# Four token tiles turned by block transposes and a trip through DRAM instead of by TensorE, in a decoder layer on one core

## The chip, the core and the metric

The kernel runs on one core of a Trainium2 chip. The metric is the time of one execution on the device in microseconds (us); it is the median of several runs, all on the same chip. The profile is of one further execution of the same program, taken by the hardware profiler. Engines are named as in the profile: PE is TensorE's matmul, PEld its loading of weights, DVE is VectorE, ACT is ScalarE, POOL is GpSimd and SP is SyncE, which in this kernel issues most transfers.

## The reference

One layer over 1040 tokens (16 meta tokens and 1024 others) of width 1024, all in float32. The part around the change is the end of the token mixing and the start of the FFN:

```python
mixed = jax.nn.sigmoid(g_attn) * y_attn + jax.nn.sigmoid(g_conv) * y_conv
h = layer_norm(DEEPNORM_ALPHA * h + mixed @ w_out, ln1_g, ln1_b)
up = causal_dwconv(h @ ffn_w_up, ffn_dw, ffn_dw_b)
u, g = jnp.split(up, 2, axis=-1)
f = (jax.nn.gelu(g, approximate=False) * u) @ ffn_w_down
return layer_norm(DEEPNORM_ALPHA * h + f, ln2_g, ln2_b)
```

`mixed @ w_out` and the layer norm give rows of tokens; `h @ ffn_w_up` needs the same h with the 1024 features on partitions. So every 128 x 1024 tile of tokens has to be turned between the two.

## The kernel before, in words

**Products.** Every float32 matmul is made of three matmuls of a high and a low part (`product`, lines 325, 329 and 330). The FFN's two large products are formed by a scheme of seven products over 2 x 2 blocks, so the inputs of `h @ ffn_w_up` are sums and differences of four quadrants of h: DVE forms them (line 1285), ACT casts the high part of each (line 1276), and DVE subtracts to get the low part (line 1281).

**The w_out stage** is a loop over eight token tiles in the order 3, 7, 2, (-1), 6, 0, 4, 1, 5, where -1 is a pair of tokens at the edge. `out_rows(i)` makes the two halves of 512 columns of tile i: 24 matmuls into a PSUM bank `ps_w`, then on DVE the residual is added (line 1339) and half of the layer norm's statistics is taken (line 1340). After the second half come the statistics (lines 261, 268 on ACT, 276 to 278) and the normalising (line 1361). The rows are stored to `h1d`, since the last layer norm needs them; they live in two buffers of `RT` (the first half of `OB`), and the rows of h for the next tile (`h0d`) are loaded into the buffer that has come free.

**The turn.** `turn(i)` is called while a later tile is in its matmuls: eight PE transposes of 128 x 128 (line 1375) go into two PSUM banks behind the last matmul of a given half (`behind=[last]` fixes that place on PE), and eight ACT instructions (line 1385) take each 128 x 128 block out of PSUM, scale and shift it by the layer norm's gain and bias, and put it into its place of `FA`. Tile 3 is turned after the second half of tile 7, and each other tile after the first half of the tile behind it: tile 7 in tile 2, tile 2 in tile 6, tile 6 in tile 0, tile 0 in tile 4, tile 4 in tile 1, tile 1 in tile 5, and tile 5 after the stage. Below, "turn 4" is the turning of tile 4, and so on.

**Interleaved work.** The first weights of the FFN are split in the same stretch (ACT line 1405, DVE line 1406, sums on DVE line 1423), and the quadrants of the second half of the tokens (tiles 2, 3, 6, 7) are summed from tile 0 on. Every engine takes its instructions strictly in the order in which they stand in its program. That order is written: `line` chains DVE's work from tile 0 on, `rank` gives priorities, `after` pins single instructions.

**SP's queue** holds, in this stretch, a load of `h0d` and a store of `h1d` for each tile, two loads of four-byte pieces for the edge, and the weights. SP waits in its queue for what a transfer needs, and whatever is behind waits too.

Of the kernel before, what the change touches and what calls it, by code (L numbers as in the profile page):

```python
# [23 lines left out]
F = mybir.dt.float32  # L24
R = mybir.dt.float32r
AF = mybir.ActivationFunctionType
# [3 lines left out]
P = 128  # L30
D = 1024
KC = D // P
# [92 lines left out]
def tile_hybrid_layer(  # L125
# [3 lines left out]
    nc = tc.nc  # L129
    PSUM = bass.MemoryType.PSUM  # L130

    def dram(ap, offset, dims):
        return bass.AP(tensor=ap.tensor, offset=ap.offset + offset, ap=[list(d) for d in dims])

    def load(o, i):
        return nc.sync.dma_start(out=o, in_=i)
# [5 lines left out]
    def f32(ap):  # L142
        return ap.bitcast(F)

    def after(ins, first):

        tc.add_manual_dep(ins.ins, first.ins.name, mybir.DependencyInfo(
            mybir.DependencyClass.NoSync, mybir.DependencyReason.SCHED_ONLY), reason="order of work")

    @contextmanager  # L150
    def rank(p):

        saved = tc.cur_priority
        tc.cur_priority = p
        yield
        tc.cur_priority = saved
# [19 lines left out]
    h0d = dpool.tile([U, D], F, name="h0d")  # L176
# [1046 lines left out]
    def h1F(sub, h, k):  # L1223
        o = h1_at(sub, h * KC + k)
        return FA[:, o:h1_at(sub, h * KC + k + 1)]
# [85 lines left out]

    WO_ORDER = (4, 5, 0, 1, 2, 3, 6, 7)
    edge = const.tile([P, KC, 2], F, name="edge")
    r_next = [1]

    def out_rows(i, between=(), work=()):


        n, u = (P, 2 + i * P) if i >= 0 else (2, 0)
        if n == P:  # L1320
            o = r_next[0] % 2 * 1024
            r_next[0] += 1
            whole = RT[:, o:o + 1024]
            load(whole, h0d[u:u + n, :])
        else:
            whole = OB[:, 3072:4096]
        r = whole[:n]
        order = WO_ORDER if i != 5 else (0, 1, 2, 3, 6, 7, 4, 5)
        turned = None
        st = small.tile([P, 2, 6], F, name="st")  # L1330
        pin = line if i in (0, 4, 1, 5) else lambda ins: ins
        for half in range(2):
            hs = slice(half * 512, half * 512 + 512)
            ps = pat.tile([P, 512], F, name="ps_w", tag="mm", bufs=3)
            if n == P:
                last = product(ps, [(mixed(i, k, 0), mixed(i, k, 1), wo[k][0][:, hs], wo[k][1][:, hs])
                                    for k in order], turned)
                with rank(RK_TURN):
                    pin(nc.vector.tensor_tensor(r[:, hs], ps, r[:, hs], OP.add))
                    pin(nc.vector.bn_stats(st[:, half], r[:, hs]))  # L1340
                turned = None
                if between[half:] and between[half]:
                    turned = turn(*between[half], behind=[last])
                if half == 0:
                    for f, *x in work:
                        f(*x)
                continue

            for j in range(4):
                nc.tensor.matmul(ps[:2], sel[:, j // 2 * 2:j // 2 * 2 + 2], two_parts[j // 2][j % 2][:, hs],  # L1350
                                 start=j == 0, stop=j == 3)
            nc.scalar.copy(r[:, hs], ps[:2])
        if n < P:
            q = FA[:2, 0:1024]
            load(q, h0d[0:2, :])
            nc.vector.tensor_tensor(r, r, q, OP.add)
        with rank(RK_TURN):
            (mu, rs), = ln_stats([(r, n)], half_stats=st if n == P else None)
            for a in (512, 0) if i == 5 else (None,):
                x = r if a is None else r[:, a:a + 512]  # L1360
                ins = pin(nc.vector.tensor_scalar(x, x, mu, rs, OP.subtract, OP.mult))
        if n == P:
            load(h1d[u - 2:u - 2 + P, :], r)
        else:
            load(ed, r)
            for t in range(2):
                load(edge[:, :, t], dram(ed, t * D, [[1, P], [P, KC]]))
        return whole, n, ins

    def turn(i, r, n, ins, banks=None, behind=None, upper=False):  # L1370
        with rank(RK_TURN):
            for j, k0 in enumerate((4, 0) if upper else (0, 4)):
                ps = banks[j] if banks else pat.tile([P, 512], F, name="ps_h", tag="s", bufs=2)
                for k in range(4):
                    ins = nc.tensor.transpose(ps[:, k * P:(k + 1) * P], r[:, (k0 + k) * P:(k0 + k + 1) * P], ident)
                    if behind:
                        after(ins, behind[-1])
                        behind.append(ins)
                for k in range(k0, k0 + 4):
                    src = ps[:, (k - k0) * P:(k - k0 + 1) * P]  # L1380
                    h, jj = divmod(i, 4)
                    sub = 0 if jj < 2 else 1
                    a = 2 + jj * P - SUB[sub][0]
                    dst = h1F(sub, h, k)[:, a:a + P]
                    nc.scalar.activation(dst, src, AF.Identity, bias=b1col(k), scale=g1col(k))
        return behind[-1] if behind else None


    RING = [RHO[:, i * 1024:(i + 1) * 1024] for i in range(4)]
    RING += [None] * 4  # L1390
# [85 lines left out]
            5: [(w_first, 6)]}  # L1476
    for i in (3, 7, 2, -1, 6, 0, 4, 1, 5):
        if i == -1:
            out_rows(i)
            continue  # L1480
        rows = out_rows(i, ahead, work.get(i, ()))
        ahead = [None, (i, *rows)] if i == 3 else [(i, *rows)]
        if i == 3:
            two_rows(7, rows[2])
        if i == 7:
            for a, (hi, lo) in zip(two_sum, two_parts):
                after(split(a, hi, lo, True), rows[2])
            two_stack.close()
            W2.append(wo_stack.enter_context(tc.tile_pool(name="w2", bufs=1, side="right", reuse_waits="tile")).tile(
                [P, 2048], R, name="W2"))  # L1490
        if i == 0:
            form_t2(1)
        if i == 4:
            split_of(1, BT4)
            split_of(1, BT1)
            edges()
        if i == 1:
            split_of(1, BT3)
            split_of(0, B21, EARLY)
            form_t3(0, EARLY)  # L1500
            form_t4(0, EARLY)
# [427 lines left out]
```

## Time and profile before

| | |
|---|---|
| median of 3 runs | 1234.82 us (1234.75 to 1234.85) |
| the profiled execution's own time | 1234.65 us |
| its span, first to last instruction | 1232.9 us |
| PE busy, share of the span | 1223.6 us, 99% |
| DVE busy | 1084.5 us, 88% |
| ACT busy | 584.4 us, 47% |
| the w_out stage in the trace | about 500 to 588 us |
| granted TensorE clock, mean | 0.998 |

The profiled execution's time is 1.75 us longer than its span, and 0.17 us below the median. In a timeline, a row gives the start, the duration, the engine, the line, what is written from what, how many instructions are merged in the row, and in square brackets how long the engine had been idle and what ended that. Durations of instructions that follow one another on an engine overlap a little, so the distance of two starts is what one costs. The program's names for tiles: `ps_w` and `ps_h` are PSUM banks, `OB`, `FA`, `OC`, `RHC`, `RHO`, `OA` are large buffers in SBUF, `wr` are raw weights.

### The profile page before, as it was taken

What the parts mean: (1) busy time and instruction counts of PE and PEld (TensorE: products, weight loads), DVE (VectorE), ACT (ScalarE), POOL (GpSimd) and SP (SyncE); (2) the same over time, 40 slices, a digit from 0 to 9 for tenths busy, and PEclk for the clock granted to TensorE, in tenths of its full rate; (3) what the DMA queues carried; (4) which work ended last, traced back from release to release, by engine and by line L of the source; (5) the groups of instructions that cost most, each with busy time, mean ns of one, the idle gap of its engine ahead of it and who ended that gap; (6) DMA issues with size and microseconds to landing.
All of it is one profiled execution on the core that took longest, in us unless ns stands there. A gap on an engine that the chain in (4) does not pass through costs nothing.

```text
span 1232.9 us, 21777 instructions
## 1 busy us (share of the span) xinstructions
PE 1223.6 (99%) x8564; PEld 1141.3 (93%) x8564; DVE 1084.5 (88%) x1840; ACT 584.4 (47%) x1065; POOL 15.0 (1%) x19
## 2 busy tenths in 40 slices
PE   9999999999999999999999999999999999999997
PEld 8999999999999999888999999999999998888886
DVE  8899989999879798659899999998999986995697
ACT  7532346654265233435655545555455553544331
POOL 1000000000000010000000000000000000000000
PEclk9999999999999999999999999999999999999999
DMA  7284834412255544322255555554465568997722
GB/s 280 74 277 101 213 96 112 129 55 73 85 153 175 180 140 136 116 73 87 69 182 197 193 191 197 191 187 137 167 210 190 182 230 305 395 334 295 255 87 86
DMA packets 104726, 210.62 MB, mean 171 GB/s; under 512 B 28520, under 2 KB 42394, under 8 KB 104624
## 3 DMA queue, kind: packets, MB, share of 16 engines
q1 hardware_dynamic: 88624, 198.16, 48.6%
q10 hardware_dynamic: 16000, 11.07, 2.9%
q8 instruction: 67, 1.10, 0.4%
q14 instruction: 35, 0.29, 0.1%
HBM read 147.59 MB, written 60.38 MB: 169 GB/s over the span
## 4 chain that ended last, share of the span: by engine, by line
PE 98%; DVE 1%; ACT 0%; issue 0%; DMA 0%; POOL 0%; DVEq 0%; POOLq 0%
PE px L1596 14%; PE py L1596 9%; PE ps_x L1742 9%; PE ps_z L330 8%; PE ps_z L329 8%; PE ps_z L325 8%; PE ps_z L1742 8%; PE pw L1596 5%; PE pz L1596 5%; PE ps_p L325 2%; PE ps_p L329 2%; PE ps_p L330 2%; PE ps_w L329 2%; PE ps_w L330 2%; PE ps_w L325 2%; PE ps_z L565 2%
## 5 line engine op out<-in xcount | busy, mean ns | idle before, releaser
L715 DVE SCALAR_TENSOR_TENSOR FA<-cin,cols,FA 128x1026 f32<-128x1026 f32 x120 | 152.3, 1278 | 0.9
L330 PE MATMUL ps_z<-RHO,wlo 128*128 128x256 f32 (+2 forms) x324 | 103.6, 320 | 0.0
L329 PE MATMUL ps_z<-RHO,whi 128*128 128x256 f32 (+2 forms) x324 | 103.5, 319 | 0.0
L330 PE MATMUL ps_z<-RHC,wlo 128*128 128x256 f32 (+2 forms) x324 | 103.4, 319 | 0.0
L329 PE MATMUL ps_z<-RHC,whi 128*128 128x256 f32 (+2 forms) x324 | 103.4, 319 | 0.0
L325 PE MATMUL ps_z<-RHC,whi 128*128 128x256 f32 (+2 forms) x324 | 103.2, 319 | 0.0
L325 PE MATMUL ps_z<-RHO,whi 128*128 128x256 f32 (+2 forms) x324 | 103.2, 318 | 0.0
L294 ACT CAST whi<-wr 128x1024 fp32r<-128x1024 f32 x37 | 38.9, 1051 | 107.4 <-PE ps_z L329 85.1
L1405 ACT CAST RHO<-wr 128x512 fp32r<-128x512 f32 x92 | 55.3, 619 | 26.2 <-DMA wr<-in_w_up_dram 12.2
L1406 DVE TENSOR_TENSOR RHO<-wr,RHO 128x512 fp32r<-128x512 f32 x92 | 62.4, 690 | 5.2 <-ACT RHO L1405 4.9
L325 PEld LDWEIGHTS ps_z<-RHO,whi 128*128 128x128 f32 x324 | 60.9, 188 | 4.5
L329 PEld LDWEIGHTS ps_z<-RHO,whi 128*128 128x128 f32 x324 | 60.9, 188 | 4.2
L325 PEld LDWEIGHTS ps_z<-RHC,whi 128*128 128x128 f32 x324 | 60.9, 188 | 4.1
L329 PEld LDWEIGHTS ps_z<-RHC,whi 128*128 128x128 f32 x324 | 61.0, 188 | 4.1
L330 PEld LDWEIGHTS ps_z<-RHO,wlo 128*128 128x128 f32 x324 | 61.0, 188 | 4.0
L330 PEld LDWEIGHTS ps_z<-RHC,wlo 128*128 128x128 f32 x324 | 61.0, 188 | 3.9
L1423 DVE TENSOR_TENSOR wr<-wr 128x512 f32<-128x512 f32 x88 | 60.9, 692 | 0.2
L297 DVE TENSOR_TENSOR wlo<-wr,whi 128x1024 fp32r<-128x1024 f32 x35 | 42.7, 1221 | 12.0 <-ACT whi L294 11.6
L1608 ACT COPY FA<-px 128x514 f32<-128x514 f32 (+2 forms) x23 | 13.1, 569 | 71.1 <-PE px L1596 71.0
L1405 ACT CAST ws<-wr 128x512 fp32r<-128x512 f32 x60 | 36.1, 618 | 20.9 <-DVE wr L1423 11.8
L722 ACT ACTIVATE FA<-ps_z,cols 128x258 f32<-128x258 f32 (+2 forms) x48 | 26.1, 543 | 39.4 <-PE ps_z L330 39.0
L1406 DVE TENSOR_TENSOR ws<-wr,ws 128x512 fp32r<-128x512 f32 x60 | 40.6, 688 | 3.6 <-ACT ws L1405 3.5
(487 smaller groups left out, 3492.2 us busy)
## 6 DMA issues: line engine op xcount, KB each, us to landing
wr<-in_w_up_dram SPq DMA_DIRECT2D x44, 512.0 KB
wr<-in_w_z_dram SPq DMA_DIRECT2D x30, 512.0 KB
fd<-FA SPq DMA_DIRECT2D x44, 256.0 KB
OB<-in_w_down_dram SPq DMA_DIRECT2D x19, 512.0 KB
qt<-qd SPq DMA_DIRECT2D x28, 256.0 KB
td<-OB SPq DMA_DIRECT2D x12, 512.0 KB
sums<-fd SPq DMA_DIRECT2D x12, 512.0 KB
sd<-sums SPq DMA_DIRECT2D x12, 512.0 KB
```

What stands on the lines that cost most here:

```text
L294: ins = nc.scalar.copy(hi, raw)
L297: return (nc.vector if quick else nc.gpsimd).tensor_tensor(lo, raw, f32(hi), OP.subtract)
L325: ins = nc.tensor.matmul(ps, ah, bh, start=i == 0, stop=False)
L329: nc.tensor.matmul(ps, ah, bl, start=False, stop=False)
L330: last = nc.tensor.matmul(ps, al, bh, start=False, stop=i == n - 1)
L715: nc.vector.scalar_tensor_tensor(acc[c], cin[:, j:j + U], wc, acc[c], OP.mult, OP.add)
L722: nc.scalar.activation(t, ps, AF.Tanh, bias=bcol(14 + i), scale=0.5)
L1405: nc.scalar.copy(hi, src)
L1406: ins = nc.vector.tensor_tensor(lo, src, f32(hi), OP.subtract)
L1423: ins = nc.vector.tensor_tensor(*x)
L1596: ins = nc.tensor.matmul(o, x[:, ks], bmat(sub, q, hl, k), start=first and k + j == 0, stop=k == 3 and j == 2, skip_group_check=not first)
L1742: nc.tensor.matmul(bank[:, cs], l[:, ts], r[:, ws], start=first and a and x + k == 0, stop=z and x == len(ops) - 1 and k == 2, skip_group_ ...
```

## The change

Four of the eight tiles (3, 7, 2 and 0) are no longer turned by PE. For each of them

- DVE turns every 32 x 32 block inside its own 32 partitions (one `transpose` over 128 x 1024, line 1414 of the changed kernel) from the row buffer into a second buffer `blocks`; for tile 0 this instruction is part of DVE's written order (`line`);
- SP stores `blocks` to a DRAM scratch `bd` (128 rows of 4 KB), and loads it back in four transfers, each into 32 partitions and in runs of 256 floats, so that the blocks come to the partitions where they belong; the place (`TURN_AT`) is an unused piece of `OC`, for tile 0 of `RHC`;
- eight ACT instructions (line 1437) scale, shift and place the blocks, from SBUF now. `shifted` keeps them in their written order; ACT's stand at a place in the loop that was chosen by hand (`turn_in`).

Tiles 6, 4, 1 and 5 are still turned by PE. All loads of rows, stores of rows and block transfers of this stretch are now queued on SP in a written order (`in_turn`, `fetch`, `NEXT_ROWS`).

```diff
+    NROW = (3, 7, 2, 6, 0, 4, 1, 5)
+    NEXT_ROWS = dict(zip(NROW, NROW[2:]))
+    moves, fetched = [], {}
+    def in_turn(ins):
+        if moves:
+            after(ins, moves[-1])
+        moves.append(ins)
+    def fetch(i):
+        o = (NROW.index(i) + 1) % 2 * 1024
+        fetched[i] = RT[:, o:o + 1024]
+        in_turn(load(fetched[i], h0d[2 + i * P:2 + (i + 1) * P, :]))
...
-            load(whole, h0d[u:u + n, :])
+            if i not in fetched:
+                fetch(i)
+            if not moves[1:]:
+                fetch(NROW[1])
+            whole = fetched[i]
...
                     turned = turn(*between[half], behind=[last])
+                    if between[half][0] in NEXT_ROWS:
+                        fetch(NEXT_ROWS[between[half][0]])
...
-            load(h1d[u - 2:u - 2 + P, :], r)
+            in_turn(load(h1d[u - 2:u - 2 + P, :], r))
...
+    TURN_AT = {3: (OC, 4144, 2048), 7: (OC, 5168, 2048), 2: (OC, 6192, 2048), 0: (RHC, 2096, 3072)}
+    TURN_N = list(TURN_AT)
+    bd = dpool.tile([len(TURN_N), P, D], F, name="bd")
+    def turn_dma(i, r, norm):
+        t, o, b = TURN_AT[i]
+        blocks, cols = OB[:, b:b + 1024], f32(t[:, o:o + 1024])
+        with rank(RK_TURN):
+            ins = nc.vector.transpose(blocks.rearrange("p (q k j) -> p q k j", q=4, k=KC),
+                                      r.rearrange("p (k q j) -> p q k j", k=KC, q=4))
+            after(ins, norm)
+            if i in (0, 4):
+                line(ins)
+            in_turn(load(bd[TURN_N.index(i)], blocks))
+            if i in NEXT_ROWS:
+                fetch(NEXT_ROWS[i])
+            for q in range(4):
+                in_turn(load(cols[32 * q:32 * q + 32].rearrange("p (a c) -> p a c", a=4),
+                             dram(bd, TURN_N.index(i) * P * D + 256 * q, [[D, 32], [32 * D, 4], [1, 256]])))
+    shifted = []
+    def turn_in(i, norm=None):
...
+            for k in range(KC):
+                ins = nc.scalar.activation(h1F(sub, h, k)[:, a:a + P].rearrange("p (a j) -> p a j", a=4), src[:, k],
+                                           AF.Identity, bias=b1col(k), scale=g1col(k))
+                if shifted:
+                    after(ins, shifted[-1])
...
         if i == -1:
-            out_rows(i)
+            turn_in(7, out_rows(i)[2])
             continue
         rows = out_rows(i, ahead, work.get(i, ()))
-        ahead = [None, (i, *rows)] if i == 3 else [(i, *rows)]
+        ahead = [] if i in TURN_AT else [(i, *rows)]
+        if i in TURN_AT:
+            turn_dma(i, rows[0], rows[2])
+        j = {7: 3, 6: 2, 4: 0}.get(i)
+        if j in TURN_AT:
+            turn_in(j, rows[2] if j else None)
```

**ACT, around tile 0's columns, before.** `FA<-ps_h` are the eight instructions that take turn 0 out of PSUM; `RHO<-wr` are casts of FFN weights, `OC<-FA`, `OC<-OB` and `RHC<-FA` casts of quadrants, `sd<-mv` a tile's statistics (tile 0's first, tile 4's last).

```order
L268 ACTIVATE sd<-mv,eps 128x1
L1276 CAST OC<-FA 128x1024
L1385 ACTIVATE FA<-ps_h,cols 128x128 x8
L1276 CAST OC<-OB 128x1024
L1405 CAST RHO<-wr 128x512 x3
L1276 CAST RHC<-FA 128x1024
L268 ACTIVATE sd<-mv,eps 128x1
```

The same place now; `FA<-RHC` are the eight instructions that read what the four loads have brought for tile 0.

```order
L268 ACTIVATE sd<-mv,eps 128x1
L1276 CAST OC<-FA 128x1024
L1276 CAST OC<-OB 128x1024
L1461 CAST RHO<-wr 128x512
L1437 ACTIVATE FA<-RHC,cols 128x128 x8
L1461 CAST RHO<-wr 128x512 x2
L1276 CAST RHC<-FA 128x1024
L268 ACTIVATE sd<-mv,eps 128x1
```

The eight have moved behind the second cast of a quadrant and the first of three casts of weights; the other two casts of weights stay behind them.

**DVE, from tile 0's normalising to the second half of tile 4, before.** The first row normalises tile 0; the two rows `OB<-ps_w` add the two halves of tile 4.

```order
L1361 TENSOR_SCALAR OB<-OB,mv,sd 128x1024
L1285 TENSOR_TENSOR FA<-FA 128x1024
L1285 TENSOR_TENSOR OB<-FA 128x1024
L1339 TENSOR_TENSOR OB<-ps_w,OB 128x512
L1340 BN_STATS st<-OB 128x6
L1406 TENSOR_TENSOR RHO<-wr,RHO 128x512
L1423 TENSOR_TENSOR wr<-wr 128x512 x3
L1281 TENSOR_TENSOR OC<-OB,OC 128x1024
L1406 TENSOR_TENSOR RHO<-wr,RHO 128x512
L1285 TENSOR_TENSOR FA<-OB,FA 128x1024
L1339 TENSOR_TENSOR OB<-ps_w,OB 128x512
```

The same place now:

```order
L1378 TENSOR_SCALAR OB<-OB,mv,sd 128x1024
L1414 STREAM_TRANSPOSE OB<-OB 128x1024
L1285 TENSOR_TENSOR FA<-FA 128x1024
L1285 TENSOR_TENSOR OB<-FA 128x1024
L1352 TENSOR_TENSOR OB<-ps_w,OB 128x512
L1353 BN_STATS st<-OB 128x6
L1462 TENSOR_TENSOR RHO<-wr,RHO 128x512
L1479 TENSOR_TENSOR wr<-wr 128x512 x3
L1281 TENSOR_TENSOR OC<-OB,OC 128x1024
L1462 TENSOR_TENSOR RHO<-wr,RHO 128x512
L1285 TENSOR_TENSOR FA<-OB,FA 128x1024
L1352 TENSOR_TENSOR OB<-ps_w,OB 128x512
```

One instruction has come in, the block transpose, and nothing else has changed its place. The second `RHO<-wr,RHO` needs the second of the three casts of weights on ACT.

**SP, around tile 0, now** (before, a store of `h1d` and a load of `h0d` alternate here). `bd` is the scratch; the first store of `h1d` is tile 0's, and `OB<-h0d` brings the rows of tile 1.

```order
L136 DMA h1d<-OB 128x1024
L136 DMA bd<-OB 128x1024
L136 DMA OB<-h0d 128x1024
L136 DMA RHC<-bd 32x4x256 x4
L136 DMA h1d<-OB 128x1024
```

Six transfers stand where two stood, and the rows of the next tile stand ahead of the four loads.

More of the change, by code (lines that the diff above doesn't have):

```diff
@@ L1313, in tile_hybrid_layer @@
     edge = const.tile([P, KC, 2], F, name="edge")
-    r_next = [1]
+    NROW = (3, 7, 2, 6, 0, 4, 1, 5)
[9 more added lines that the diff above has]
+        in_turn(load(fetched[i], h0d[2 + i * P:2 + (i + 1) * P, :]))
     def out_rows(i, between=(), work=()):
@@ L1320, in out_rows @@
         if n == P:
-            o = r_next[0] % 2 * 1024
-            r_next[0] += 1
-            whole = RT[:, o:o + 1024]
-            load(whole, h0d[u:u + n, :])
+            if i not in fetched:
[3 more added lines that the diff above has]
+            whole = fetched[i]
         else:
@@ L1351, in out_rows @@
                                  start=j == 0, stop=j == 3)
-            nc.scalar.copy(r[:, hs], ps[:2])
+            ins = nc.scalar.copy(r[:, hs], ps[:2])
+            after(ins, shifted[-1])
+            shifted.append(ins)
         if n < P:
@@ L1362, in out_rows @@
         if n == P:
-            load(h1d[u - 2:u - 2 + P, :], r)
+            in_turn(load(h1d[u - 2:u - 2 + P, :], r))
         else:
-            load(ed, r)
+            in_turn(load(ed, r))
             for t in range(2):
@@ L1386, in turn @@
         return behind[-1] if behind else None
+    TURN_AT = {3: (OC, 4144, 2048), 7: (OC, 5168, 2048), 2: (OC, 6192, 2048), 0: (RHC, 2096, 3072)}
[18 more added lines that the diff above has]
+    def turn_in(i, norm=None):
+        t, o, b = TURN_AT[i]
+        cols = f32(t[:, o:o + 1024])
+        with rank(RK_TURN):
+            h, jj = divmod(i, 4)
+            sub = 0 if jj < 2 else 1
+            a = 2 + jj * P - SUB[sub][0]
+            src = cols.rearrange("p (a k j) -> p k a j", a=4, k=KC)
+            for k in range(KC):
+                ins = nc.scalar.activation(h1F(sub, h, k)[:, a:a + P].rearrange("p (a j) -> p a j", a=4), src[:, k],
+                                           AF.Identity, bias=b1col(k), scale=g1col(k))
+                if shifted:
+                    after(ins, shifted[-1])
+                if norm is not None and k == 0:
+                    after(ins, norm)
+                shifted.append(ins)
     RING = [RHO[:, i * 1024:(i + 1) * 1024] for i in range(4)]
```

## The prediction

> **What bounds the kernel now.** I read the page first, for the engine that sets the end, and then the timelines of PE, DVE, ACT and SP in the w_out stage.
>
> ```profile
> PE 1223.6 (99%) x8564; PEld 1141.3 (93%) x8564; DVE 1084.5 (88%) x1840; ACT 584.4 (47%) x1065; POOL 15.0 (1%) x19
> ...
> PE 98%; DVE 1%; ACT 0%; issue 0%; DMA 0%; POOL 0%; DVEq 0%; POOLq 0%
> ```
>
> The first row is busy time, the second the chain of work that ended last. PE is busy for 99% of the span and holds 98% of the chain. Taking work from PE therefore pays in full, as long as PE does not come to wait for someone.
>
> PE's timeline around turn 4 shows both what a turn costs and how PE goes on behind it:
>
> ```profile
> 569.31 0.40 PE L330 MATMUL ps_w<-whi,RHO 128*128 128x512 f32 x1
> 569.55 1.04 PE L1375 MATMUL ps_h<-cols,OB 128*128 128x128 f32 x8
> 570.34 0.48 PE L325 MATMUL ps_w<-RX,RHO 128*128 128x512 f32 x1
> 570.66 0.40 PE L329 MATMUL ps_w<-RX,RHO 128*128 128x512 f32 x1
> 570.89 0.39 PE L330 MATMUL ps_w<-RX,RHO 128*128 128x512 f32 x1
> ```
>
> Matmuls of 512 columns start every 0.23 us. From the start of the turn to the third matmul behind it are 1.34 us, where two matmuls alone take 0.45: a turn costs PE 0.89 us. There is no gap ahead of it, so tile 4's rows were ready when PE came. The question is by how much. DVE's timeline tells it; the row's last field is the idle time before it.
>
> ```profile
> 548.71 2.35 DVE L1281 TENSOR_TENSOR OC<-FA,OC 128x1024 fp32r<-128x1024 f32 x2
> 550.98 1.22 DVE L1281 TENSOR_TENSOR RHC<-FA,RHC 128x1024 fp32r<-128x1024 f32 x1
> 552.53 0.69 DVE L1339 TENSOR_TENSOR OB<-ps_w,OB 128x512 f32<-128x512 f32 x1 [0.32 <-PE ps_w L330]
> ...
> 555.14 0.81 DVE L1361 TENSOR_SCALAR OB<-OB,mv,sd 128x1024 f32<-128x1024 f32 x1
> 555.87 1.22 DVE L1285 TENSOR_TENSOR FA<-FA 128x1024 f32<-128x1024 f32 x1
> ...
> 562.43 1.22 DVE L1281 TENSOR_TENSOR OC<-OB,OC 128x1024 fp32r<-128x1024 f32 x1
> 563.83 0.69 DVE L1406 TENSOR_TENSOR RHO<-wr,RHO 128x512 fp32r<-128x512 f32 x1 [0.18 <-ACT RHO L1405]
> ...
> 565.58 0.69 DVE L1339 TENSOR_TENSOR OB<-ps_w,OB 128x512 f32<-128x512 f32 x1
> ...
> 568.18 0.81 DVE L1361 TENSOR_SCALAR OB<-OB,mv,sd 128x1024 f32<-128x1024 f32 x1
> ```
>
> The last row normalises tile 4 and ends at 568.99; turn 4 starts at 569.55, a margin of 0.56 us. From 548.71 to there the rows have two idle times, of 0.32 and 0.18 us; beside them DVE only waits for ACT's part of the statistics in each tile's own chain. So here PE is only just the bound: DVE, fed by ACT, is right behind it. Before tile 0 it is otherwise: of the stage's eight waits of DVE for `ps_w`, those behind tiles 3, 7, 2 and 6 are up to 4.9 us long.
>
> ```profile
> DVE OB L1339 <- PE ps_w L330: 20.1, 8, 4.9
> ```
>
> **What is removed.** Four turns of eight transposes, 4 x 0.89 = 3.6 us of PE. Three of them (3, 7 and 2) stand ahead of tile 0, so PE comes to tile 0 2.7 us earlier, and to turn 4 at 569.55 - 3.6 = 566.0. If nothing else moved, the kernel would take 3.6 us less.
>
> **What is added, where it is covered.** The block transpose is not in the trace; 128 x 1024 values on DVE cost 0.81 (L1361, one input) to 1.22 us (L1285, two inputs). I take 1.2 us. For tiles 3, 7 and 2 it and the DRAM trip lie in the stretch in which DVE waits for PE, and nothing needs their columns before the casts of quadrants behind tile 6. I cost them at nothing on DVE; without that cover it would be 3.6 us. The rows of the next tiles stay early enough, since each is loaded one tile ahead.
>
> ACT takes the blocks from SBUF; again no row has that. Out of PSUM eight cost 2.90 us:
>
> ```profile
> 542.43 0.29 ACT L268 ACTIVATE sd<-mv,eps 128x1 f32<-128x1 f32 x1 [2.81 <-DVE mv L261]
> 546.62 2.90 ACT L1385 ACTIVATE FA<-ps_h,cols 128x128 f32<-128x128 f32 x8 [3.90 <-PE ps_h L1375]
> 549.55 1.05 ACT L1276 CAST RHC<-FA 128x1024 fp32r<-128x1024 f32 x1
> 550.50 0.62 ACT L1405 CAST RHO<-wr 128x512 fp32r<-128x512 f32 x1
> ...
> 588.69 1.14 ACT L1405 CAST ws<-wr 128x512 fp32r<-128x512 f32 x2 [2.20 <-DMA wr<-in_w_up_dram]
> ...
> 605.30 0.81 ACT L1520 ACTIVATE FA<-FA,cols 128x512 f32<-128x512 f32 x1 [1.53 <-DVE RX L1281]
> ```
>
> L1520 is the same operation from SBUF at four times the width and takes 0.81, so eight cost between 2.9 and 6.5 us; I take 3.2, near the first, as the width is the same.
>
> **What moves: DVE at tile 0.** ACT's eight for tile 2 now stand behind tile 6's statistics, 542.43 - 2.7 = 539.8, and end at 543.1. Then follow a cast of a quadrant (about 1.0, to 544.1), turn 6 out of PSUM (2.75, to 546.8), and the second cast, to 547.8. DVE's second L1281 starts there (before at 548.71 + 2.35 - 1.22 = 549.84); the third waits for a cast of weights and a cast of a quadrant (0.5 and 1.05, to 549.4) and ends at 550.5. So DVE adds tile 0's second half at 550.5, where it was 552.53: 2.0 us earlier, not 2.7. Tile 0 is normalised 2.61 + 0.81 us later, at 553.9, and its blocks are turned at 555.1.
>
> **The DRAM trip of tile 0.** These are SP's rows of a store of 512 KB, of the load that waits for it, and of a load for which ACT waits at 588.69:
>
> ```profile
> 544.18 0.33 SPq L136 DMA_DIRECT2D h1d<-OB  x1
> 547.05 0.33 SPq L136 DMA_DIRECT2D OB<-h0d  x1
> ...
> 585.20 0.33 SPq L136 DMA_DIRECT2D wr<-in_w_up_dram  x1
> ```
>
> A store lands 2.87 us after its issue, a load 3.49. The rows of tile 0 are stored at 554.0 and land at 556.9; then SP issues the fetch of tile 1's rows, which lands at 560.4. The blocks are stored at 555.2 and land at 558.1; only then are the four loads issued. They share the queue with the fetch. If they ran beside it, they would land at 558.1 + 3.49 = 561.6; if their bytes come behind it, they need their own time on the engines as well, which two windows give:
>
> ```profile
> 480.00:485.00 5.00, 5.00 (x46) 5.00 (x45) 4.65 (x11) 2.73 (x4) 2.40 (x1) 1.00 0.41 108
> 585.00:589.00 4.00, 4.00 (x25) 3.53 (x24) 1.83 (x4) 1.80 (x4) 0.00 (x0) 1.00 0.39 131
> ```
>
> The DMA share is the column before the last. One load of 512 KB in rows of 4 KB holds the engines for 0.39 x 4 = 1.6 us; two loads with rows of 1 KB, as the blocks have, that together carry 512 KB, for 0.41 x 5 = 2.0. So 560.4 + 1.9 = 562.3 us, and I take this.
>
> **Who waits.** ACT's eight for tile 0 run from 562.3 to 565.5. Behind them in ACT's order are two casts of weights (1.14, L1405), to 566.7. DVE's second L1406 needs the second cast: it starts at 566.7 where it was 563.83. DVE itself would have been there at 562.9 (before: 563.65 without its wait; 2.0 earlier through the second half, 1.2 later through the transpose). So DVE stands for 3.8 us. Behind it on DVE are the second half of tile 4 and its normalising, which ends 568.99 - 563.83 = 5.16 us later, at 571.9. On PE, turn 4 waits for that, and all matmuls behind it with it. It was at 569.55: **2.35 us late**, though PE arrived 3.6 us early. It stands for 571.9 - 566.0 = 5.9 us. Behind turn 4 the order is that of before and PE leads again, so nothing gives the 2.35 back.
>
> **The clock.** The row of PE's last matmuls, and then two windows with the granted clock (third column from the right):
>
> ```profile
> 1225.08 0.52 PE L1742 MATMUL ps_z<-RHO 128*128 128x256 f32 x3
> ```
>
> ```profile
> 1225.00:1228.00 3.00, 0.60 (x5) 0.39 (x4) 2.19 (x6) 1.01 (x4) 0.00 (x0) 0.98 0.22 83
> 1228.00:1232.90 4.90, 0.00 (x0) 0.00 (x0) 1.71 (x3) 0.26 (x1) 0.00 (x0) 0.50 0.29 107
> ```
>
> PE ends at 1225.6, and the clock is at half from about 1227.9, 2.3 us later (0.02 x 3 us lost at half rate is the last 0.1 us of the window). A pause of 5.9 us is longer than that. How long the half clock then lasts is not in the trace. Between nothing (it comes back at once) and 5.4 us (the whole half tile behind turn 4 at half speed), I take 2.3 us of half clock, the time that the fall took: **1.15 us**. The Trainium skill, "TensorE: Matmul & The Clock Gate", Part 1, says that the clock falls after an idle window of 3.4 us which runs freely, and comes back after about as long of sustained work. By that the clock would fall in most pauses of 5.9 us, not in all, and the price would be 1.7 us, a time of 1238.9; the fall within 2.3 us above is quicker than its rule.
>
> **Sum.** + 2.35 + 1.15 = + 3.5 us on the profiled execution's 1234.65 gives 1238.15. The median of the runs is 0.17 above that execution, so 1238.3.
>
> **Rivals.**
> (B) The clock stays up. Then + 2.35 remains, 1237.2; with loads that land at 561.6 and eight at 2.9 us, it is + 1.35. For it: the trace has no pause inside the kernel. Against: the fall at the end after 2.3 us.
> (C) Not slower: the blocks land early enough for ACT. DVE's slot for the second L1406 is 562.9, less two casts and the eight: they would have to land by 558.6, half a microsecond after their store does. Then DVE's own chain decides, 2.0 us earlier and 1.2 later: - 0.8, 1234.0. Against: no load of the trace is nearly as quick. For: my 555.1 is a chain of small steps.
> (D) The block loads are slow: each goes to 32 partitions, a shape that this stretch does not have. At twice the engine time they land at 564.3, and turn 4 is 4.3 us late; with the clock, 1240.3, and up to 1243 with a longer half clock.
> (E) Full gain: turn 4 is not late at all and PE stays the bound, - 3.6, 1231.2. It needs DVE 2.9 us earlier at tile 4 than its chain gives.
> The Trainium skill, "VectorE: DVE Perf Modes", section "The three transpose paths", warns that a plain DMA with strides is 19 times slower than the transposing one. The 32 x 32 blocks are turned on DVE here, and a run is 1 KB; by the 1 KB rows above I do not expect that. Were it so, the loads would take tens of microseconds.
>
> **How the numbers follow.** Forecast 0.50, B 0.22, C 0.10, D 0.13, E 0.05. A measurement of this kernel can tell about 0.2%, 2.5 us, from no change. E and a little of C are faster: 0.07. Most of C and more than half of B are within 2.5 us: 0.22. The rest is slower: 0.71. The range leaves out C, E and the last of D: its lower end is B at its cheapest with something off, 1235.3, its upper end D with a longer half clock, 1243.0.
>
> **What would show it.** In the changed kernel's profile: the four loads for tile 0 are issued about 3 us after their store; ACT waits there for a DMA at about 561 to 563; DVE has an idle row of 3 to 5 us before the second `RHO<-wr,RHO` of that stretch, put down to ACT; PE has a gap of 5 to 7 us ahead of turn 4, and a granted clock under 1.0 around 570 to 575. If ACT does not wait for that DMA, the working is wrong at the DRAM trip. If PE's gap is there and the clock stays at 1.00, B holds. If PE's gap stands at another turn, I have the wrong place. A time under 1234 would say that the whole chain is not there.

## The result and the profile after

The changed kernel takes 1241.82 us (median of 6 runs, 1240.38 to 1242.25), the kernel before 1234.80 in runs beside it: ratio 1.0055, 95% interval 1.0044 to 1.0065. It is 7.0 us slower, twice the 3.5 that were forecast, and inside the range. The profiled execution took 1242.21 us (span 1240.4), 7.56 more than that of before (1234.65); the sums below are made against these two.

The page, in the same two rows:

```profile
PE 1222.5 (99%) x8532; PEld 1139.8 (92%) x8532; DVE 1088.7 (88%) x1844; ACT 585.8 (47%) x1065; POOL 15.0 (1%) x19
...
PE 92%; DVE 2%; ACT 2%; DMA 2%; issue 1%; SPq 0%; POOL 0%; DVEq 0%; ACTq 0%; POOLq 0%
```

PE has 32 matmuls less and is still busy for 99% of the span, but the chain that ended last now leaves PE: 6% of it lies on DVE, ACT and DMA, which had 1% before. PE's timeline shows where:

```profile
565.75 0.39 PE L330 MATMUL ps_w<-whi,RHO 128*128 128x512 f32 x1
574.96 1.94 PE L1392 MATMUL ps_h<-cols,OB 128*128 128x128 f32 x8 [8.83 <-DVE OB L1378]
576.55 0.77 PE L325 MATMUL ps_w<-RX,RHO 128*128 128x512 f32 x1
577.13 0.63 PE L329 MATMUL ps_w<-RX,RHO 128*128 128x512 f32 x1
577.55 0.63 PE L330 MATMUL ps_w<-RX,RHO 128*128 128x512 f32 x1
```

PE arrives at turn 4 at 566.1 (forecast: 566.0), stands for 8.83 us (forecast: 5.9) and turns tile 4 at 574.96, which is 5.41 us later than the 569.55 of before. The rows behind are slow as well: matmuls of 512 columns start every 0.42 us instead of 0.23. Two windows, one of the pause and one of the turn and what follows, have the granted clock in the third column from the right:

```profile
566.00:569.60 3.60, 0.13 (x1) 0.00 (x0) 0.00 (x0) 3.60 (x9) 0.00 (x0) 1.00 0.00 0
569.60:580.00 10.40, 5.04 (x16) 4.38 (x17) 9.61 (x17) 4.38 (x12) 0.00 (x0) 0.51 0.14 53
```

The clock is at half from 569.7 to 579.9, so 5.0 us of it lie behind the start of turn 4. Of the 7.56 us, 5.41 are turn 4's lateness; the other 2.15 have appeared by the end behind it.

The chain of waits, from tile 2's blocks to turn 4 (start, duration, what):

```profile
532.92 4.88 DMA bd<-OB
...
537.82 0.32 SPq L136
...
542.13 3.19 ACT FA L1437 x8
...
557.35 2.65 DMA bd<-OB
...
560.02 0.32 SPq L136
...
565.41 3.19 ACT FA L1437 x8
568.60 1.03 ACT RHO L1461 x2
...
569.66 0.69 DVE RHO L1462
...
574.00 0.82 DVE OB L1378
...
574.96 1.94 PE ps_h L1392 x8
```

From 557.35 on these are the links that the prediction named, in its order: the store of the blocks, the loads (the first is issued at 560.02), ACT's eight, the two casts of weights behind them, the second `RHO<-wr,RHO` on DVE, tile 4's normalising, turn 4. Above them stands a wait that it did not have: the trip of tile 2. (Around tile 0, seven transfers stand where two stood, not the six that were counted: two stores, the fetch of rows and four loads.) From the store's issue to that of the first load are 4.90 us for tile 2 and 2.67 for tile 0; from the first load's issue to ACT's first use, 4.31 and 5.39.

ACT's timeline shows its wait for tile 2, in the brackets:

```profile
539.78 0.30 ACT L268 ACTIVATE sd<-mv,eps 128x1 f32<-128x1 f32 x1 [5.63 <-DVE mv L261]
542.13 3.19 ACT L1437 ACTIVATE FA<-OC,cols 128x128 f32<-128x128 f32 x8 [2.06 <-DMA OC<-bd]
```

ACT was free for tile 2's eight at 540.1 and got the columns 2.06 us later. DVE's timeline has the consequences, first at the quadrants and then at the cast of weights:

```profile
550.01 1.23 DVE L1281 TENSOR_TENSOR OC<-FA,OC 128x1024 fp32r<-128x1024 f32 x1 [2.49 <-ACT OC L1276]
551.48 1.23 DVE L1281 TENSOR_TENSOR RHC<-FA,RHC 128x1024 fp32r<-128x1024 f32 x1 [0.24 <-ACT RHC L1276]
552.62 0.68 DVE L1352 TENSOR_TENSOR OB<-ps_w,OB 128x512 f32<-128x512 f32 x1
...
569.66 0.69 DVE L1462 TENSOR_TENSOR RHO<-wr,RHO 128x512 fp32r<-128x512 f32 x1 [4.67 <-ACT RHO L1461]
```

Tile 0's second half is added at 552.62, as late as before (552.53), although PE had it ready earlier.

### The profile page after: what moved, and what is told of

Same layout as the page of the kernel before. It is cut to its first block, busy times and chain, and to the rows that moved or that the text cites. A ratio compares the mean times of both kernels' runs of the same rounds, so it can differ in the third digit from the quotient of the medians.

```text
span 1240.4 us, 21759 instructions
## 1 busy us (share of the span) xinstructions
PE 1222.5 (99%) x8532; PEld 1139.8 (92%) x8532; DVE 1088.7 (88%) x1844; ACT 585.8 (47%) x1065; POOL 15.0 (1%) x19
## 4 chain that ended last, share of the span: by engine, by line
PE 92%; DVE 2%; ACT 2%; DMA 2%; issue 1%; SPq 0%; POOL 0%; DVEq 0%; ACTq 0%; POOLq 0%
PE px L1657 14%; PE py L1657 9%; PE ps_x L1803 9%; PE ps_z L330 8%; PE ps_z L329 8%; PE ps_z L325 8%; PE ps_z L1803 8%; PE pw L1657 5%; PE pz L1657 5%; PE ps_p L325 2%; PE ps_p L329 2%; PE ps_p L330 2%; PE ps_z L565 2%; PE ps_o L925 1%; PE ps_s L876 1%; PE ps_t L912 1%
## 5 line engine op out<-in xcount | busy, mean ns | idle before, releaser
L1657 PE MATMUL px<-OA,RHO 128*128 128x258 f32 (+1 forms) x336 | 43.6, 279 | 0.0
```

The lines of the kernel that those rows point to most:

```text
L1657: ins = nc.tensor.matmul(o, x[:, ks], bmat(sub, q, hl, k), start=first and k + j == 0, stop=k == 3 and j == 2, skip_group_check=not first)
```

## The experiments

The theory after these rows: the loss starts at two waits of ACT for block loads, reaches turn 4 through ACT's and DVE's written orders, and the half clock behind PE's pause adds about 2 us. The rivals: DVE's own added work and PE's earliness make turn 4 late whatever ACT does; tile 2's trip is covered and all comes from tile 0's; the half clock costs nothing that counts. In each kernel, turn 4's start is compared with 569.55 (before), and the time of the profiled execution with 1234.65. The experiments ran in three groups, each beside the kernel before, which took 1234.68, 1234.63 and 1234.69 us there; the ratios are to these. One profiled execution stands beside the median of several runs, and it isn't always near it: that of "tiles 3, 7, 0" (1241.38) is the slowest of its four.

| kernel | median of runs, us | turn 4 at | later than before | profiled time, later than before |
|---|---|---|---|---|
| the change | 1241.82 | 574.96 | 5.41 | 7.56 |
| ACT's eight for tile 0 later | 1237.03 | 570.12 | 0.57 | 2.78 |
| the same, PE kept busy | 1235.18 | 569.97 | 0.42 | 0.51 |
| the change, PE kept busy | 1240.71 | 573.73 | 4.18 | 4.20 |
| tile 0 alone by DMA | 1242.10 | 575.10 | 5.55 | 6.67 |
| tiles 3, 7, 0 by DMA | 1239.80 | 573.15 | 3.60 | 6.73 |
| loads of tile 0 ahead of the fetch | 1240.65 | 573.85 | 4.30 | 5.44 |
| no trip | 1234.42 | 568.09 | -1.46 | -1.17 |
| tiles 3, 7, 2 by DMA | 1233.95 | 568.54 | -1.01 | -0.59 |
| tiles 3, 7, 2, loads ahead of the fetch | 1234.49 | 568.23 | -1.32 | -1.00 |
| tiles 3, 7 by DMA | 1232.97 | 567.74 | -1.81 | -1.64 |

**ACT's eight for tile 0 behind tile 4's normalising.**

```diff
-            turn_in(j, rows[2] if j else None)
+            turn_in(j, rows[2])
```

> ACT's eight for tile 0 stand behind tile 4's normalising instead of ahead of two casts of weights; all transfers, transposes and turns stay. Theory (the trip of tile 0 delays turn 4 only through ACT's order): DVE's second RHO<-wr,RHO starts at 565.0, straight behind the L1281 that ends there, and turn 4 at 570.3 instead of 574.96 (before: 569.55). PE's pause shrinks from 8.8 to 4.2 us, so the clock may still fall at its end: 1235.4 us without a fall, up to 1237.8 with one. Rival (DVE cannot deliver tile 4 earlier, whatever ACT does, since its own work grew and PE came too early): turn 4 stays within 1 us of 574.96 and the time at 1241 or more.

Measured: 1237.03 us (11 runs, 1235.74 to 1237.85), ratio to before 1.0017 (1.0008 to 1.0026). DVE no longer has an idle row ahead of the second `RHO<-wr,RHO`:

```profile
563.69 1.22 DVE L1281 TENSOR_TENSOR OC<-OB,OC 128x1024 fp32r<-128x1024 f32 x1
564.82 0.68 DVE L1462 TENSOR_TENSOR RHO<-wr,RHO 128x512 fp32r<-128x512 f32 x1
```

All transfers and transposes are still there; only what stood behind a waiting instruction has moved. Turn 4 is back by 4.84 us, to 570.12. So the wait on ACT, and not DVE's own work, makes the larger part of turn 4's lateness. In the profiled execution, 1237.43 us, PE still pauses 3.85 us and the clock still falls. It did not cost the same in all runs: the five with a mean granted clock of 0.995 or 0.996 took 1237.04 to 1237.85 us, the six with 0.997 or 0.998 took 1235.74 to 1237.03.

**Tile 0 by PE again.**

```diff
-    TURN_AT = {3: (OC, 4144, 2048), 7: (OC, 5168, 2048), 2: (OC, 6192, 2048), 0: (RHC, 2096, 3072)}
+    TURN_AT = {3: (OC, 4144, 2048), 7: (OC, 5168, 2048), 2: (OC, 6192, 2048)}
```

> Tile 0 is turned by PE again; tiles 3, 7 and 2 still go through DRAM. Theory: nobody waits for a trip of tile 0; DVE adds tile 0's second half at 552.6 as now (before: 552.53), has no block transpose there, and turn 4 comes at 569.65, 0.1 us later than before, though PE arrives 2.7 us earlier. PE pauses 2.8 us, too short for the clock to fall. So the three turns taken from PE gain nothing: 1234.9 us, within 0.1% of before. Rival (the removal of PE work pays in full once nothing waits): 2.7 us less than before, 1232.1.

Measured: 1233.95 us (11 runs, 1233.22 to 1235.20), ratio 0.9995 (0.9986 to 1.0004), no difference that can be told. The loss is gone and three turns less on PE, 2.7 us, give no gain that shows, as the theory said. Turn 4 came 1.1 us earlier than expected, at 568.54: the expectation forgot the margin of 0.56 us between tile 4's normalising and turn 4, of which 0.15 pass in the changed kernel too (574.81 to 574.96); tile 0's second half was added at 552.21 and not 552.6; and DVE's chain from there on was 0.3 us shorter. PE waits 0.85 us there, behind DVE. So the 2.8 us that the expectation calls too short for a fall of the clock did not come about, and other rows speak against it: with ACT's eight later, the clock fell 2.2 us after PE's last matmul.

**Tile 0 alone by DMA.**

```diff
-            after(ins, shifted[-1])
-            shifted.append(ins)
...
-    TURN_AT = {3: (OC, 4144, 2048), 7: (OC, 5168, 2048), 2: (OC, 6192, 2048), 0: (RHC, 2096, 3072)}
+    TURN_AT = {0: (RHC, 2096, 3072)}
...
-            turn_in(7, out_rows(i)[2])
+            out_rows(i)
...
-        ahead = [] if i in TURN_AT else [(i, *rows)]
+        ahead = [] if i in TURN_AT else [None] * (i == 3) + [(i, *rows)]
```

The lines beside `TURN_AT` take tile 7's eight out of ACT's order and put turn 3 back to its place of before.

> Only tile 0 goes through DRAM; tiles 3, 7 and 2 are turned by PE. Theory: the whole loss hangs on tile 0. Its rows are normalised at 556.0 in before and in the changed kernel, so turn 4 is as late as there, at about 574.9; PE arrives at 568.7, pauses 6.2 us and the clock falls: about 1242, as with all four tiles. Rival (the loss comes from PE running ahead of DVE through three turns less, or from the traffic of four trips): 1236 or less.

Measured: 1242.10 us (4 runs, 1241.32 to 1243.01), ratio 1.0062 (1.0046 to 1.0077). Turn 4:

```profile
575.10 1.94 PE L1390 MATMUL ps_h<-cols,OB 128*128 128x128 f32 x8 [6.31 <-DVE OB L1376]
```

One tile of four carries the whole loss (L1390 is the line of the turn here). The other three trips, taken together with the three turns that they spare PE, neither add to it nor take from it, and the volume of traffic is not the cause.

**Tile 2 by PE again.**

```diff
-    TURN_AT = {3: (OC, 4144, 2048), 7: (OC, 5168, 2048), 2: (OC, 6192, 2048), 0: (RHC, 2096, 3072)}
+    TURN_AT = {3: (OC, 4144, 2048), 7: (OC, 5168, 2048), 0: (RHC, 2096, 3072)}
```

> Tile 2 is turned by PE again; tiles 3, 7 and 0 go through DRAM. Theory (of the lateness of turn 4, about 2 us come from tile 2's trip, which ends after ACT wants its columns, the rest from tile 0's): tile 0's second half is added at 550.75 instead of 552.62, and turn 4 comes 1.9 us earlier than with all four tiles, at 573.1. PE arrives at 567.0, pauses 6.1 us, the clock falls: 1239.2 to 1240.6. Rival (tile 2's trip is covered, all comes from tile 0's): turn 4 at 575, 1241 to 1242.

Measured: 1239.80 us (4 runs, 1239.21 to 1241.38), ratio 1.0043 (1.0029 to 1.0057). Turn 4 starts at 573.15, as expected, and tile 0's second half is added when PE has it:

```profile
550.76 0.69 DVE L1352 TENSOR_TENSOR OB<-ps_w,OB 128x512 f32<-128x512 f32 x1 [0.32 <-PE ps_w L330]
```

With one PE turn more, everything from there to turn 4 is 1.8 us earlier than in the changed kernel. So tile 2's trip is not covered; together with "tile 0 alone" this says why three trips more bring nothing: what they give PE, tile 2's wait on ACT takes back.

**No trip.** `turn_in` reads `blocks`; the store and the loads are left out.

```diff
-            in_turn(load(bd[TURN_N.index(i)], blocks))
...
-            for q in range(4):
-                in_turn(load(cols[32 * q:32 * q + 32].rearrange("p (a c) -> p a c", a=4),
-                             dram(bd, TURN_N.index(i) * P * D + 256 * q, [[D, 32], [32 * D, 4], [1, 256]])))
...
-        cols = f32(t[:, o:o + 1024])
+        cols = OB[:, b:b + 1024]
```

> DVE's block transposes and ACT's eight stay where they are, but the stores and loads of the blocks are left out: ACT reads the blocks where DVE put them, so that the features land on other partitions. Theory (the trips, not DVE's added work, make the loss): ACT never waits for a DMA; tile 2's eight run at 540.1, tile 0's second half at 550.5, tile 0's transpose costs DVE 1.2 us, turn 4 comes at 568.2 and PE pauses 2.1 us: 1233.3. Rival (DVE's transposes or the missing cover of PE matter most): turn 4 after 570, 1235 or more.

Measured: 1234.42 us (10 runs, 1233.31 to 1235.15), ratio 0.9998 (0.9988 to 1.0007). Turn 4:

```profile
568.09 1.06 PE L1392 MATMUL ps_h<-cols,OB 128*128 128x128 f32 x8 [1.93 <-DVE OB L1378]
```

The profiled execution, 1233.48, is where it was expected; the runs spread over 1.8 us and their median is 1.1 higher, which no row explains. Without the trips, of the 3.6 us taken from PE only 1.46 are left at turn 4, since DVE, not PE, then decides there. The trips themselves cost the rest, 7.4 us between the two medians.

**The loads of tile 0 ahead of the fetch of tile 1's rows.**

```diff
-            if i in NEXT_ROWS:
+            if i in NEXT_ROWS and i != 0:
                 fetch(NEXT_ROWS[i])
             for q in range(4):
...
+            if i == 0:
+                fetch(NEXT_ROWS[i])
```

> The change as it is, with one order changed on SP: for tile 0 the four block loads are issued ahead of the fetch of tile 1's rows. Theory (the loads' bytes run behind those of the fetch): the store still lands about 2.7 us after its issue, but ACT's eight start about 4.1 us after the first load's issue instead of 5.4, and turn 4 comes 1.2 us earlier, at 573.8: 1240.5, if the clock falls as before. Rival (the loads take 5.4 us from issue to use anyway, by their own shape): turn 4 unchanged within 0.3 us, 1241.8.

Measured: 1240.65 us (4 runs, 1240.09 to 1241.53), ratio 1.0050 (1.0034 to 1.0065). SP's rows and ACT's, whose lines are two later here:

```profile
557.34 0.32 SPq L136 DMA_DIRECT2D bd<-OB  x1
559.98 1.75 SPq L136 DMA_DIRECT2D RHC<-bd  x4
```

```profile
564.30 3.18 ACT L1439 ACTIVATE FA<-RHC,cols 128x128 f32<-128x128 f32 x8 [1.20 <-DMA RHC<-bd]
```

From the first load to its use are 4.32 us instead of 5.39: the fetch in front costs the loads 1.1 us, and turn 4 moves by as much, to 573.85. What is left, 4.32, the four loads take with no fetch ahead of them. SP issues them one after the other within 1.75 us; the single load of 512 KB in the kernel before took 3.49.

**PE kept busy in its pause.** In the changed kernel 34 matmuls, and with ACT's eight later 15, into the bank that turn 4 overwrites.

```diff
+                for k in range(34 if i == 4 and j == 0 else 0):
+                    ins = nc.tensor.matmul(ps, mixed(1, k % 8, 0), wo[k % 8][0][:, 0:512], start=True, stop=True)
+                    after(ins, behind[-1])
+                    behind.append(ins)
                 for k in range(4):
                     ins = nc.tensor.transpose(ps[:, k * P:(k + 1) * P], r[:, (k0 + k) * P:(k0 + k + 1) * P], ident)
```

> All of the change stays; 34 matmuls of 512 columns are added ahead of turn 4, 7.7 us of PE work, into the bank that turn 4 then overwrites. Theory (clock): they fit into PE's pause of 8.8 us, turn 4 still starts at 575.0, the granted clock stays at 1.00, and the kernel with more work is faster by the price of the half clock, about 2.4 us: 1239.8. Rival (the half clock costs nothing that counts, for instance as DVE is behind anyway): 1241 to 1242, as without them.

Measured: 1240.71 us (5 runs, 1238.82 to 1240.86), ratio 1.0042 (1.0030 to 1.0055). A window of 8 us from turn 4's start, in the changed kernel:

```profile
574.96:582.96 8.00, 8.00 (x29) 6.75 (x30) 7.28 (x12) 4.77 (x11) 0.00 (x0) 0.69 0.39 134
```

and with the added matmuls:

```profile
573.73:581.73 8.00, 8.00 (x41) 6.76 (x41) 7.90 (x13) 5.01 (x11) 0.00 (x0) 1.00 0.36 132
```

The clock stays at 1.00, 41 matmuls run in the window instead of 29 (the eight transposes counted), and the end is as late as turn 4 is (4.20 and 4.18), with nothing behind it. The medians differ by 1.1 us only, less than expected, and turn 4 itself moved: in this execution tile 2's store landed 1.6 us earlier than in the changed kernel's. The five runs fall in two groups, 1238.82 and 1238.85, and 1240.71 to 1240.86; the profiled execution is one of the first. So the second pair, in which turn 4 stays in its place, is the cleaner one.

> As the run with ACT's eight behind tile 4's normalising, with 15 matmuls of 512 columns (3.4 us of work) added in PE's pause of 3.85 us ahead of turn 4. Theory (the half clock after a pause costs half of the time that it lasts beyond the pause): turn 4 stays at 570.1, the clock at 1.00, and the 5.2 us of half clock behind turn 4, 2.2 us of time, are gone: 1235.2, with less spread between runs than the 1235.7 to 1237.9 without the added matmuls. Rival (the clock is not what makes that kernel slower than before): 1237 as without.

Measured: 1235.18 us (11 runs, 1234.30 to 1235.66), ratio 1.0002 (0.9994 to 1.0011). Turn 4 is where it was without the added matmuls (569.97 against 570.12), the clock does not fall, and the median is 1.85 us lower, by work that is thrown away. The 1.85 is an average over runs in which the low clock cost more and less.

**Three tiles, block loads ahead of the fetch.** Tiles 3, 7 and 2, with the fetch behind the four loads for each.

```diff
             in_turn(load(bd[TURN_N.index(i)], blocks))
-            if i in NEXT_ROWS:
-                fetch(NEXT_ROWS[i])
             for q in range(4):
...
+            if i in NEXT_ROWS:
+                fetch(NEXT_ROWS[i])
```

> Tiles 3, 7 and 2 through DRAM, and SP issues a tile's four block loads ahead of the fetch of the next rows instead of behind it. Theory (the store of the blocks lands late since the fetch's bytes are in the queues with it): tile 2's store lands 2.9 us after its issue instead of 4.6, its loads are issued at 535.8 instead of 537.4, ACT's eight start at 540.1 without a wait (now 541.73), and turn 4 comes when PE does, 567.7: 1232.9 to 1233.3. Rival (the store's landing has nothing to do with the fetch): loads at 537.4 or later, turn 4 as without this edit at 568.5, 1234, or worse as the next rows come late.

Measured: 1234.49 us (11 runs, 1233.65 to 1237.40), ratio 1.0002 (0.9993 to 1.0011). This settles little. SP's rows for tiles 7 and 2:

```profile
521.48 0.38 SPq L136 DMA_DIRECT2D bd<-OB  x1
528.07 1.75 SPq L136 DMA_DIRECT2D OC<-bd  x4
...
533.39 0.32 SPq L136 DMA_DIRECT2D bd<-OB  x1
536.59 1.97 SPq L136 DMA_DIRECT2D OC<-bd  x4
```

Tile 2's store now lands within 3.2 us instead of 4.6, and ACT's wait for its columns shrinks from 1.69 to 0.28 us. But tile 7's first load is issued 6.6 us after its store, where it was 4.1 in the changed kernel; a fetch of rows is now issued right ahead of that store, at 520.54. That fetch brings tile 2's rows, and DVE waits for them:

```profile
525.58 0.69 DVE L1352 TENSOR_TENSOR OB<-ps_w,OB 128x512 f32<-128x512 f32 x1 [4.23 <-DMA OB<-h0d]
```

Without the edit this row stands at 521.29, without a wait. At tile 0's first half, 0.84 us of it are left (544.33 against 543.49), and ACT comes to tile 2's columns later by as much, so that it starts on them only 0.57 us earlier. The rival's last condition, that the next rows come late, has occurred. The median is not lower than without this edit, and the spread is the widest of all.

**Tiles 3 and 7 alone by DMA.**

```diff
-    TURN_AT = {3: (OC, 4144, 2048), 7: (OC, 5168, 2048), 2: (OC, 6192, 2048), 0: (RHC, 2096, 3072)}
+    TURN_AT = {3: (OC, 4144, 2048), 7: (OC, 5168, 2048)}
```

> Only tiles 3 and 7 go through DRAM; 2 and 0 are turned by PE as before. Theory: both trips land long before anyone needs them, nothing is added on DVE or ACT behind tile 6, and what was in step before (ACT's turn 6, DVE's chain, turn 4) all moves with PE: tile 0's second half at 552.53 - 1.78 = 550.75, turn 4 at 567.8, no pause on PE there: 1234.65 - 1.78 = 1232.9, up to 1233.3 if a part is given back later in the stage. Rival (DVE's chain is the bound around turn 4 and does not move): turn 4 at 569.0 or later, 1234 or more.

Measured: 1232.97 us (11 runs, 1232.70 to 1233.84), ratio to before 0.9986 (0.9977 to 0.9995). DVE's rows of tile 0's second half and of the second `RHO<-wr,RHO`:

```profile
550.72 0.69 DVE L1352 TENSOR_TENSOR OB<-ps_w,OB 128x512 f32<-128x512 f32 x1 [0.32 <-PE ps_w L330]
...
562.03 0.69 DVE L1462 TENSOR_TENSOR RHO<-wr,RHO 128x512 fp32r<-128x512 f32 x1 [0.19 <-ACT RHO L1461]
```

They are the rows of before with their idle times (0.32 and 0.18), 1.8 us earlier. Turn 4 follows at 567.74 without a gap. Two turns less pay in full there, 2 x 0.89, and 1.64 of it reach the end. This version is 1.7 us faster than the kernel before, by a clear interval though by less than the 0.2% of the prediction, and 8.9 us faster than the change.

## Why the prediction was right, and which terms were too small

The sign held, and so did the mechanism for tile 0: a late trip, carried to turn 4 by ACT's and DVE's orders, and a half clock behind PE's pause. What failed is that tile 2's trip is covered, and two terms were too small. The time lies inside the range partly by luck: its upper end was meant for slow loads with a longer half clock, while 2.1 us of the lateness came from tile 2, to whose trip no rival gave a price. Point by point:

- **The removal**: PE came to turn 4 at 566.1, forecast 566.0. Right.
- **The block transpose**: forecast 1.2 us, measured 1.25 (1.17 to the next start). **ACT's eight from SBUF**: forecast 3.2, measured 3.19. Right.
- **"For tiles 3, 7 and 2 it and the DRAM trip lie in the stretch in which DVE waits for PE"**: the step that failed, for tile 2. Its four block loads were needed at 540.1 and came at 542.1. The prediction priced tile 0's trip from rows, but not tile 2's, which it only called covered. By its own bounds, a store of 2.87 us and 4.2 from the first load to the use, tile 2's blocks (stored at 532.92) would have come at 540.0, with no margin at all. The store alone took 4.90. This cost 2.1 us at tile 0's second half (552.62 for 550.5; 550.50 without the trips), and the run with tile 2 on PE gave 1.8 of turn 4's lateness back.
- **Tile 0's trip**: store to first load 2.67 us, forecast 2.9; first load to use 5.39, forecast 4.2 (562.3 - 558.1). The forecast was 3.49 for a load alone and 0.7 for the fetch ahead of it. The run with the loads ahead of the fetch measured 4.32 and 1.07, so queueing behind the fetch was a right reason, but the larger part of the error, 0.83 of 1.19, is time that the four loads take by themselves. Tile 2's loads, whose fetch was issued 3.4 us before them, took 4.31. Together: 565.41 - 562.3 = 3.1 = 2.15 (blocks stored at 557.35, not 555.2) - 0.23 + 1.19.
- **Who waits**: ACT's two casts, DVE's second `RHO<-wr,RHO` (idle for 4.67 us, forecast 3.8), tile 4's normalising, turn 4: every link is in the chain. DVE needed 5.16 us from there to the end of the normalising by the prediction, and 574.81 - 569.66 = 5.15 in the trace. Turn 4 is 5.41 us late instead of 2.35; the difference is the 3.1 of the trips.
- **The clock**: it did halve; the price was 2.15 us, forecast 1.15. The half clock lasted 5.0 us behind the start of turn 4, not the 2.3 that were taken from the time of the fall. That time was no measure for how long it lasts. (The prediction's upper bound, 5.4 us for a half tile, is that half tile's time at full clock; at half it would be twice as long.) The rule from the Trainium skill, "TensorE: Matmul & The Clock Gate", Part 1, gave 1.7 and was nearer, though in the five traces with a fall the price lay between 1.12 and 3.13, so no single figure could be right. The pair of medians with and without added matmuls gave 1.85, at a pause of 3.85 us.
- **Rivals**: (B) fell, as the clock fell in every trace with a pause of 3.85 us or more that was not filled. (C)'s reason, DVE's own chain, is what decides without the trips, at 1234.42 us; its sum left out the margin of 0.56 us between tile 4's normalising and turn 4. With it turn 4 comes up to 1.35 us early, at 568.2, and not 0.8; 568.09 was measured. (D) was half right: the loads were slower than forecast, by 1.2 us and not by twice their engine time, and 0.83 of it without a fetch ahead; whether by their shape or by being four was not tested. Loads of tens of microseconds did not occur; the longest of the trips took 9.2. (E) did not occur at any number of tiles; by the prediction's own numbers it needed DVE 2.2 us earlier (568.2 to 566.0), not 2.9.
- **What would show it**: the loads were issued 2.67 us after their store, DVE's idle row was 4.67 us and the clock low from 569.7 on, as named. ACT's wait ended at 565.41, past the 561 to 563, and PE's gap was 8.83 us, past the 5 to 7.

## What to carry to other kernels

When a transfer takes the place of work on the busiest engine, price the round trip for each place where its result is used, from rows of that stretch, against the moment at which the using engine is free; "covered" is a number too. What decides is less the transfer than what is queued behind the instruction that waits for it: moving eight instructions in ACT's order gave back 4.8 of 7.0 us. And choose how many pieces to move by the slack behind each: two tiles with slack gained, and the third and fourth took more than they gave.

## What the runs showed of the hardware

The low clock lasted for whole steps, in every trace that had it. In the changed kernel (slices of 0.2 us; the clock is the third column from the right):

```profile
569.60:569.80 0.20, 0.00 (x0) 0.00 (x0) 0.14 (x1) 0.03 (x1) 0.00 (x0) 0.74 0.00 0
...
579.80:580.00 0.20, 0.20 (x2) 0.20 (x1) 0.04 (x1) 0.20 (x2) 0.00 (x0) 0.66 0.00 0
```

and with ACT's eight later:

```profile
568.40:568.60 0.20, 0.00 (x0) 0.00 (x0) 0.02 (x1) 0.20 (x2) 0.00 (x0) 0.62 0.00 0
...
575.20:575.40 0.20, 0.20 (x2) 0.13 (x1) 0.00 (x0) 0.20 (x1) 0.00 (x0) 0.81 0.00 0
```

A mean of 0.74 in the first slice says that the half clock began 0.10 us before its end, at 569.70; worked out so at each edge, the clock was at half for 10.24 us in the first kernel and for 6.83 in the second, and for 6.83 in the three others where it fell (tile 0 alone, tiles 3, 7 and 0, loads ahead of the fetch). That is three times and twice 3.413 us. From the end of the low spell in the changed kernel, 579.94, to the fall behind its last matmul, 1235.30, are 655.36 us, 192 times 3.413. So in these traces the clock changes only at the edges of windows of 3.413 us, which run on whatever PE does. The Trainium skill, "TensorE: Matmul & The Clock Gate", Part 1, has such windows, 3413 ns long and free-running, and these traces agree. The same section of the Trainium skill has the clock fall after at least one idle window; here the fall came between 2.2 us (ACT's eight later) and 5.3 us (tiles 3, 7 and 0) after the end of PE's last matmul, so less than a whole idle window was enough, and the measurement decides.

These are windows of "ACT's eight later", of "tiles 3, 7, 0" and of "no trip" in which PE stopped; the figure before `(x6)` or `(x7)` is the time for which PE was busy in them:

```profile
565.04:568.45 3.41, 1.23 (x6) 0.69 (x4) 3.11 (x5) 1.25 (x2) 0.00 (x0) 1.00 0.00 0
565.55:568.96 3.41, 1.50 (x7) 0.92 (x5) 1.11 (x2) 2.26 (x6) 0.00 (x0) 1.00 0.00 0
564.61:568.02 3.41, 1.55 (x7) 0.94 (x5) 2.87 (x9) 1.35 (x2) 0.00 (x0) 1.00 0.00 0
```

Behind the first the clock fell, behind the other two it did not. It came back behind windows with PE busy for 2.86 us or more, and stayed low behind one with 2.64 (tiles 3, 7, 0). What exactly is counted in a window, these few cases don't show: at the kernels' ends, with other matmuls, the clock also fell behind windows with PE busy for up to 1.53 us (tiles 3, 7, 2).

What the low clock costs is close to half of what of it lies behind the pause: 5.0 us for 2.15, 5.2 for 2.21 (ACT's eight later), 2.9 for 1.12 (tile 0 alone), 6.05 for 3.13 (tiles 3, 7 and 0). The last two pauses are nearly the same, 6.31 and 6.11 us; the price differs by where the pause falls in the windows. The runs bear this out: of the changed kernel's six, the two with a mean granted clock of 0.996 took 1240.38 and 1241.27 us, the four with 0.994 took 1241.64 to 1242.25.

In the changed kernel the store of 512 KB of blocks landed 2.65 us after its issue for tile 0 and 4.88 for tile 2, with the same two transfers around it; with PE kept busy, tile 2's landed 3.3 us after it. What decides between these was not found.
